# Float32 products of 256 and 272 columns in attention, scores and outputs, replaced by three float32r ones of split operands

## The chip, the cores and the metric

The kernel runs on one core of a Trainium2 chip. The metric is the time of one execution on the device, in microseconds (us); lower is better. The engines are TensorE (PE, its weight loads PEld), VectorE (DVE), ScalarE (ACT), GpSimd (POOL) and SyncE (SP, which here only issues transfers). A line L180 is line 180 of the kernel.

## The reference

It is a small decoder trunk with 272 tokens (16 meta tokens and 256 of the sequence), 2048 features, 16 heads of 128 and two layers, all in float32. Layer 0 has causal attention with a learned decay, layer 1 "stick-breaking" attention over one shared K and V; each is followed by a squared-ReLU MLP of 8192 features. In short:

```python
# layer 0
q, k, v, f = split(rms_norm(h) @ fox_w_in)
s = q @ k.T * scale + cum_logf[q] - cum_logf[k]      # masked to k <= q
o = softmax(s) @ v
h = h + o @ fox_w_o;  h = h + relu(rms_norm(h) @ w_up) ** 2 @ w_down
# layer 1
k, v = split(rms_norm(h) @ w_kv);  q = rms_norm(h) @ sb_w_q
z = q @ k.T * scale                                   # masked to k < q
a = exp(log_sigmoid(z) + suffix_sum(log_sigmoid(-z)))
o = a @ v
h = h + o @ sb_w_o;  h = h + relu(rms_norm(h) @ w_up) ** 2 @ w_down
return rms_norm(h)[meta tokens left out]
```

## The kernel before

Activations lie with features on the partitions and tokens along the columns: `hT` is 128 x 16 x 272. Almost all the work is in `gemm_group`: 512 output features, made from 16 chunks of 128 input features into four PSUM tiles `acc` (one per 128 features). To keep float32's precision with the faster format float32r, each operand is split in a high part, which is float32r, and the rest, which is float32r too; a product of two operands is then three products: high by high, high by low, low by high (L180). The activations are split once, by ScalarE and VectorE, into a `Split` (tiles `x_a`, `x_m`, `x_u`, `x_kv`, `x_o`, each with `hi` and `lo`). The weights come by DMA from SP's queue in pieces of 128 x 1024 (`raw`) and are split in the same way: ScalarE writes `whi` (L220), VectorE subtracts it and writes `wlo` (L221). There are four pairs of these buffers, so the splits run ahead of the products.

In attention the products are different: they were plain float32. The heads are taken in four groups of four.

- Layer 0, each group: a `gemm_group` for q, one for k, then the scores (L397): per head one float32 product of 144 columns for the first 128 queries and one of 272 for the others, into `ps`. VectorE adds the decay and finds the minimum (L400), ScalarE takes the exponential (L403), VectorE normalizes (L407). TensorE transposes the result (L428 to L430, `pp`), VectorE copies it out (L431, `pp_sb`). Then the `gemm_group` for v; `token_major` transposes v (L330) and ScalarE copies it (L332, `v_sb`). The output product is of 256 columns for the first 128 keys (L460), 128 columns for the next (L461) and a small one for the corners (L462); `put_split` writes the result into the Split `ao` (`x_o`), with ScalarE for the high part (L351) and VectorE for the low one (L352).
- Layer 1: q for all groups first. Each group then has a `gemm_group` for k, the scores of 256 columns (L575, `pza`) and of 144 (L576, `pzb`), the logarithms and their suffix sums (`pta`, `ptb`, already float32r with the split operands `eh` and `el`), an exponential in place (`z`), the `gemm_group` for v, and output products of 256 columns (L614) and 144 (L615).

The order is not written out by hand: the tile framework schedules the instructions of each engine by its own timeline of the program, so the small products of attention stand between the products of the next `gemm_group`. Each engine then runs its queue strictly in that order, with semaphores between engines. The tiles of attention come from the pool `att`, which lies behind all others in SBUF, and their PSUM tiles from `patt` (four banks). `tmp` has the tags `relu` and `u2` of the MLP, which are free during attention.

Of the kernel before, what the change touches and what calls it, by code (L numbers as in the profile page):

```python
# [33 lines left out]
def yoco_kernel(ctx: ExitStack, tc: tile.TileContext, hT_in, gains, b_f, w_f, w_qkv0, w_o0, w_up, w_dn,  # L34
# [264 lines left out]
    def forget_gates(rstd):  # L299
# [34 lines left out]

    def packed(src, label):

# [12 lines left out]
    def put_split(sp, h, nh, t, n, src):  # L349
        hi, lo = (x[:, h:h + nh, t - sp.t0:t - sp.t0 + n] for x in (sp.hi, sp.lo))  # L350
        nc.scalar.activation(hi, src, AF.Copy)  # L351
        nc.vector.tensor_tensor(out=lo, in0=src, in1=hi.bitcast(F32), op=ALU.subtract)  # L352

    ao = Split("o0", 0)
    for g in range(4):
# [8 lines left out]
        def evac_kv(m, acc, t):  # L364
            nc.vector.tensor_tensor(out=t[:, m, :], in0=acc, in1=box["rstd"], op=ALU.mult)
# [24 lines left out]
                   after={j: (lambda j=j: decays(j)) for j in range(4)})  # L390


        for j in range(4):
            h = 4 * g + j
            ps = patt.tile([P, 512], F32, tag="patt", name=f"ps_{h}")
            for q0, o, n in ((M, 0, 144), (M + P, 144, T)):
                nc.tensor.matmul(ps[:, o:o + n], qT[:, j, q0:q0 + P], kT[:, j, :n], start=True, stop=True)  # L397
            st = att.tile([P, 4], F32, tag="st", name=f"st_{h}")
            for i, (o, n) in enumerate(((0, 144), (144, T))):
                nc.vector.tensor_tensor_reduce(out=s[:, j, o:o + n], in0=ps[:, o:o + n], in1=s[:, j, o:o + n],  # L400
                                               scale=1.0, scalar=3.0e38, op0=ALU.add, op1=ALU.min,
                                               accum_out=st[:, i:i + 1])
                nc.scalar.activation(s[:, j, o:o + n], s[:, j, o:o + n], AF.Exp, bias=st[:, i:i + 1], scale=-1.0,  # L403
                                     accum_out=st[:, 2 + i:3 + i])
            nc.vector.reciprocal(st[:, 2:4], st[:, 2:4])
            for i, (o, n) in enumerate(((0, 144), (144, T))):
                nc.vector.tensor_scalar(s[:, j, o:o + n], s[:, j, o:o + n], st[:, 2 + i:3 + i], None, op0=ALU.mult)  # L407
# [13 lines left out]

        pps = []
        for pr in range(2):
            pp_sb = att.tile([P, 2, 416], F32, tag="pp", bufs=3, name=f"pp_sb_{g}_{pr}")
            for i in range(2):
                j = 2 * pr + i
                pp = patt.tile([P, 512], F32, tag="patt", name=f"pp_{4 * g + j}")
                nc.tensor.transpose(pp[:, 0:P], s[:, j, 0:P], ident)  # L428
                nc.tensor.transpose(pp[:, P:2 * P], s[:, j, 144:144 + P], ident)
                nc.tensor.transpose(pp[:, 2 * P:3 * P], s[:, j, 144 + P:144 + 2 * P], ident)  # L430
                nc.vector.tensor_copy(pp_sb[:, i, :3 * P], pp[:, :3 * P])  # L431
            pps.append(pp_sb)


        pm = patt.tile([P, 512], F32, tag="patt", name=f"pm_{g}")
# [18 lines left out]
        nc.tensor.matmul(po[:, :64], vm_sb[:, :P], pm_sb[:, P:], start=True, stop=True)  # L454
        put_split(ao, 4 * g, 4, 0, M, po[:, :64].rearrange("p (h q) -> p h q", h=4))
        for pr in range(2):
            v_sb = token_major(vT, pr, 0, f"0_{g}_{pr}")
            po = patt.tile([P, 2, 256], F32, tag="patt", name=f"po0_{g}_{pr}")
            for i in range(2):
                nc.tensor.matmul(po[:, i, :], v_sb[:, i, 0, :], pps[pr][:, i, 0:2 * P], start=i == 0, stop=False)  # L460
# [76 lines left out]
    ao = Split("o1", M)  # L537
    for g in range(4):
        kT = att.tile([P, 4, T], F32, tag="kT", bufs=1, name=f"kT1_{g}")
        vT = att.tile([P, 4, T], F32, tag="vT", bufs=1, name=f"vT1_{g}")  # L540
        gemm_group(w_kv[2 * g], xc, 0, lambda m, acc: evac_kv(m, acc, kT))
        q = qT1[g]

# [20 lines left out]
        sc = att.tile([P, 4, M], F32, tag="sc", name=f"sc_{g}")  # L564
        nc.vector.tensor_copy(sc, pt[:, 64:128].rearrange("p (h q) -> p h q", h=4))


        z = att.tile([P, 4, 416], F32, tag="s", bufs=1, name=f"z_{g}")
        for pr in range(2):
            zp = z[:, 2 * pr:2 * pr + 2, :400]  # L570
            pa = patt.tile([P, 2, 256], F32, tag="patt", name=f"pza_{g}_{pr}")
            pb = patt.tile([P, 2, 256], F32, tag="patt", name=f"pzb_{g}_{pr}")
            for i in range(2):
                j = 2 * pr + i
                nc.tensor.matmul(pa[:, i, :], kT[:, j, 0:P], q[:, j, :S], start=True, stop=True)  # L575
                nc.tensor.matmul(pb[:, i, :144], kT[:, j, P:2 * P], q[:, j, 112:S], start=True, stop=True)  # L576
# [4 lines left out]
            e = att.tile([P, 2, 416], F32, tag="pp", bufs=3, name=f"e_{g}_{pr}")[:, :, :400]  # L581
            e_hi = att.tile([P, 2, 416], F32R, tag="pp", bufs=3, name=f"eh_{g}_{pr}")[:, :, :400]
            e_lo = att.tile([P, 2, 416], F32R, tag="pp", bufs=3, name=f"el_{g}_{pr}")[:, :, :400]
# [7 lines left out]
            nc.tensor.matmul(pa, ntri_r, e_lo[:, :, 0:256], start=False, stop=False)  # L591
            nc.tensor.matmul(pa[:, :, 112:], nones_r, e_hi[:, :, 256:400], start=False, stop=False)
            nc.tensor.matmul(pa[:, :, 112:], nones_r, e_lo[:, :, 256:400], start=False, stop=True)
            nc.tensor.matmul(pb[:, :, :144], ntri_r, e_hi[:, :, 256:400], start=True, stop=False)
            nc.tensor.matmul(pb[:, :, :144], ntri_r, e_lo[:, :, 256:400], start=False, stop=True)
# [4 lines left out]
            nc.vector.tensor_tensor(out=zp[:, :, 256:400], in0=pb[:, :, :144], in1=zp[:, :, 256:400], op=ALU.add)  # L600
            nc.scalar.activation(zp, zp, AF.Exp)

        gemm_group(w_kv[2 * g + 1], xc, 0, lambda m, acc: evac_kv(m, acc, vT))

        pv = patt.tile([P, 512], F32, tag="patt", name=f"pvc_{g}")
# [1 line left out]
        vc_sb = att.tile([P, P], F32, tag="vm_sb", bufs=1, name=f"vc_sb_{g}")  # L607
        nc.scalar.copy(vc_sb, pv[:, :P])
        for pr in range(2):
            v_sb = token_major(vT, pr, 0, f"1_{g}_{pr}")  # L610
            po = patt.tile([P, 2, 256], F32, tag="patt", name=f"po1_{g}_{pr}")
            for i in range(2):
                j = 2 * pr + i
                nc.tensor.matmul(po[:, i, :], v_sb[:, i, 0, :], z[:, j, 0:256], start=i == 0, stop=False)  # L614
                nc.tensor.matmul(po[:, i, 112:], v_sb[:, i, 1, :], z[:, j, 256:400], start=False, stop=False)  # L615
# [112 lines left out]
```

## Time and profile before

| | |
|---|---|
| Median of 3 runs | 2301.25 us (2300.02 to 2301.27) |
| The profiled execution | 2299.54 us |
| Its span, first to last instruction | 2297.6 us |
| TensorE busy | 2286.6 us |
| VectorE, ScalarE busy | 1289.7 us, 1040.8 us |
| Granted TensorE clock, mean | 0.998 |

The profile is of one execution. A busy time is the union of an engine's records. A row of instructions by form reads: line, engine, operation, tiles (out<-in), shape, count | busy us, mean ns of one | idle time before them, and what ended it. A float32 product has two records on TensorE and two weight loads. Since products are pipelined, the records of TensorE overlap, and the mean of one is its latency. The chain of waits lists, in order of time, what the end of the program hung on; equal instructions that follow each other are one piece.

### The profile page before, as it was taken

How to read it: one execution, taken by the hardware profiler on the slowest of the kernel's cores; microseconds unless marked ns; L12 is line 12 of the kernel's file. 1: busy time of each engine (PE TensorE's matmuls, PEld its weight loads, DVE VectorE, ACT ScalarE, POOL GpSimd, SP SyncE). 2: the span in 40 equal slices, each digit the busy share in tenths (PEclk: the TensorE clock that was granted, in tenths of full speed). 3: DMA queues.
4: the chain of work that ended last, by engine and by line, in shares of the span. 5: the costliest groups of instructions: out<-in, count | busy, mean ns of one | idle time of the engine just before them, and what ended most of it. 6: DMA issues, size and time to landing. Idle time of an engine off the chain costs nothing.

```text
span 2297.6 us, 44810 instructions
## 1 busy us (share of the span) xinstructions
PE 2286.6 (100%) x19022; PEld 2280.1 (99%) x19022; DVE 1289.7 (56%) x1766; ACT 1040.8 (45%) x1397; POOL 40.2 (2%) x65
## 2 busy tenths in 40 slices
PE   9999999999999999999999999999999999999998
PEld 9999999999999999999999999999999999999998
DVE  7665555655455455455566555566555555555555
ACT  6444344543344344344445444455543543543553
POOL 1000000000000000000000000000000000000000
PEclk9999999999999999999999999999999999999999
DMA  7545555555555555555555544456566666565663
GB/s 235 175 158 166 170 162 172 168 185 175 182 175 180 180 174 184 175 183 175 177 189 188 172 147 147 147 174 198 189 192 201 186 193 202 185 201 192 193 199 133
DMA packets 116904, 412.32 MB, mean 179 GB/s; under 512 B 13520, under 2 KB 16992, under 8 KB 116704
## 3 DMA queue, kind: packets, MB, share of 16 engines
q1 hardware_dynamic: 114560, 406.29, 55.0%
q8 instruction: 149, 2.44, 0.4%
q10 hardware_dynamic: 2144, 3.17, 0.4%
q14 instruction: 51, 0.42, 0.1%
HBM read 407.29 MB, written 2.11 MB: 178 GB/s over the span
## 4 chain that ended last, share of the span: by engine, by line
PE 99%; DVE 0%; ACT 0%; issue 0%; DVEq 0%; ACTq 0%
PE acc L180 96%; PE ps L397 0%; PE pv L330 0%; PE pza L575 0%; PE po L460 0%; PE po L614 0%; PE idle L61 0%; PE po L615 0%; PE pzb L576 0%; PE po L461 0%; DVE ob L670 0%; PE pf L297 0%; PE pf L296 0%; PE pta L590 0%; PE pta L591 0%; PE pp L428 0%
## 5 line engine op out<-in xcount | busy, mean ns | idle before, releaser
L221 DVE TENSOR_TENSOR wlo<-raw,whi 128x1024 fp32r<-128x1024 f32 (+1 forms) x773 | 928.9, 1217 | 742.5 <-ACT whi L220 735.9
L220 ACT ACTIVATE whi<-raw 128x1024 fp32r<-128x1024 f32 (+1 forms) x773 | 797.3, 1050 | 1008.4 <-PE acc L180 981.1
L180 PE MATMUL acc<-x_m,whi 128*128 128x272 f32 (+1 forms) x4096 | 643.1, 281 | 0.0
L180 PE MATMUL acc<-x_u,whi 128*128 128x272 f32 (+1 forms) x4096 | 642.5, 281 | 0.0
L180 PEld LDWEIGHTS acc<-x_m,whi 128*128 128x128 f32 x4096 | 566.0, 188 | 0.1
L180 PEld LDWEIGHTS acc<-x_u,whi 128*128 128x128 f32 x4096 | 565.7, 188 | 0.0
L180 PE MATMUL acc<-x_m,wlo 128*128 128x272 f32 (+2 forms) x2048 | 440.8, 281 | 0.0
L180 PE MATMUL acc<-x_u,wlo 128*128 128x272 f32 (+2 forms) x2048 | 440.8, 281 | 0.0
L180 PE MATMUL acc<-x_a,whi 128*128 128x272 f32 (+1 forms) x2048 | 359.9, 288 | 0.0
L180 PEld LDWEIGHTS acc<-x_m,wlo 128*128 128x128 f32 x2048 | 323.4, 188 | 0.0
L180 PEld LDWEIGHTS acc<-x_u,wlo 128*128 128x128 f32 x2048 | 323.3, 188 | 0.0
L180 PEld LDWEIGHTS acc<-x_a,whi 128*128 128x128 f32 x2048 | 302.0, 189 | 0.9
L180 PE MATMUL acc<-x_a,wlo 128*128 128x272 f32 (+2 forms) x1024 | 254.0, 286 | 0.0
L180 PE MATMUL acc<-x_kv,whi 128*128 128x272 f32 x1024 | 191.8, 288 | 0.0
L180 PEld LDWEIGHTS acc<-x_a,wlo 128*128 128x128 f32 x1024 | 175.8, 189 | 0.8 <-issue 0.5
L180 PE MATMUL acc<-x_o,whi 128*128 128x272 f32 (+1 forms) x1024 | 161.9, 282 | 0.0
L180 PEld LDWEIGHTS acc<-x_kv,whi 128*128 128x128 f32 x1024 | 159.7, 188 | 0.0
L180 PE MATMUL acc<-x_kv,wlo 128*128 128x272 f32 x512 | 147.5, 288 | 0.0
L180 PEld LDWEIGHTS acc<-x_o,whi 128*128 128x128 f32 x1024 | 142.0, 188 | 0.0
L255 DVE TENSOR_TENSOR hT<-acc,hT 128x272 f32<-128x272 f32 (+1 forms) x160 | 69.0, 432 | 81.9 <-PE acc L180 81.7
L180 PE MATMUL acc<-x_o,wlo 128*128 128x272 f32 (+2 forms) x512 | 110.6, 282 | 0.0
L180 PEld LDWEIGHTS acc<-x_kv,wlo 128*128 128x128 f32 x512 | 96.5, 188 | 0.0
(225 smaller groups left out, 970.0 us busy)
## 6 DMA issues: line engine op xcount, KB each, us to landing
raw<-w_up SPq DMA_DIRECT2D x256, 512.0 KB, 4.7
raw<-w_dn SPq DMA_DIRECT2D x256, 512.0 KB, 4.7
raw<-w_qkv SPq DMA_DIRECT2D x92, 512.0 KB, 4.0
raw<-w_o SPq DMA_DIRECT2D x64, 512.0 KB, 4.3
raw<-w_kv SPq DMA_DIRECT2D x64, 512.0 KB, 3.9
raw<-w_q SPq DMA_DIRECT2D x32, 512.0 KB, 5.0
fk<-f_dram ACTq DMA_DIRECT2D x4, 544.0 KB, 4.9
raw<-w_qkv SPq DMA_DIRECT2D x7, 256.0 KB, 4.7
```

Of the source, the lines that this page charges most:

```text
L180: ins = nc.tensor.matmul(*args, **kw).ins
L220: on_act = nc.scalar.activation(hp, src, AF.Copy)
L221: on_dve = nc.vector.tensor_tensor(out=lp, in0=src, in1=hp.bitcast(F32), op=ALU.subtract)
L255: nc.vector.tensor_tensor(out=hT[:, c, t0:], in0=acc, in1=hT[:, c, t0:], op=ALU.add)
```

## The change

At four places a float32 product is replaced by three float32r products of split operands (`by_parts`): the 272-column scores of layer 0, the 256-column scores of layer 1, and the 256-column output products of both layers. `split` makes the parts: the high one on ScalarE, the rest on VectorE. The smaller float32 products (144, 128, 64 and 32 columns) stay.

- Layer 0, scores: the queries of the second block are split into `q2` (a buffer of tag `pp`), and k, head by head, into the rows of `ao` that the head's output takes later.
- Layer 0, outputs: of the transposed weights, `p0` (first 128 keys, split, straight out of PSUM) and `p1` (the others, a copy, in a tile of tag `relu`) replace `pp_sb`. `token_major` gives `v0` (split) and `v1` (a copy, in a tile of tag `u2`) in place of `v_sb`.
- Layer 1, scores: k is split into `k0`, which takes the buffer of tag `vT` until v is made, and q into the rows of `ao`.
- Layer 1, outputs: the first 256 columns of `z` are split into `p0`, which takes the buffer of k (`kT`) or of the group's queries (`qT`). The tile `vT` is allocated later, and the exponentials of both pairs of heads stand in a loop of their own.
- The buffers of tag `pp` grow from 832 to 1024 columns, which moves the `att` tiles behind them; the tiles of the other pools stay where they are.

```diff
+    def split(hl, src):
+        nc.scalar.activation(hl[:, 0], src, AF.Copy)
+        nc.vector.tensor_tensor(out=hl[:, 1], in0=src, in1=hl[:, 0].bitcast(F32), op=ALU.subtract)
+
     def token_major(vT, pr, t0, label):
...
-        v_sb = att.tile([P, 2, 2, P], F32, tag="v_sb", name=f"v_sb_{label}")
-        nc.scalar.copy(v_sb, pv)
-        return v_sb
+        v0 = att.tile([P, 2, 2, P], F32R, tag="v_sb", name=f"v0_{label}")
+        v1 = tmp.tile([P, T], F32, tag="u2", name=f"v1_{label}")[:, :2 * P].rearrange("p (i d) -> p i d", i=2)
+        split(v0, pv[:, :, 0, :])
+        nc.scalar.copy(v1, pv[:, :, 1, :])
+        return v0, v1
+
+    def by_parts(out, a, b, start, stop=False):
+        for k, (i, j) in enumerate(((0, 0), (0, 1), (1, 0))):
+            nc.tensor.matmul(out, a[i], b[j], start=start and k == 0, stop=stop and k == 2)
+
+    def weighted(po, v0, p0, i):
+        by_parts(po[:, i, :], [v0[:, k, i, :] for k in range(2)], [p0[:, k, i, :] for k in range(2)], i == 0)
...
+        q2 = att.tile([P, 2, 4, P], F32R, tag="pp", bufs=3, name=f"q2_{g}")
+        split(q2, qT[:, :, M + P:])
         for j in range(4):
...
-            for q0, o, n in ((M, 0, 144), (M + P, 144, T)):
-                nc.tensor.matmul(ps[:, o:o + n], qT[:, j, q0:q0 + P], kT[:, j, :n], start=True, stop=True)
+            put_split(ao, h, 1, 0, T, kT[:, j:j + 1, :])
+            nc.tensor.matmul(ps[:, 0:144], qT[:, j, M:M + P], kT[:, j, :144], start=True, stop=True)
+            by_parts(ps[:, 144:144 + T], [q2[:, k, j, :] for k in range(2)], [ao.hi[:, h], ao.lo[:, h]], True, True)
...
-                nc.vector.tensor_copy(pp_sb[:, i, :3 * P], pp[:, :3 * P])
-            pps.append(pp_sb)
+                split(p0[:, :, i, :], pp[:, :2 * P])
+                nc.vector.tensor_copy(p1[:, i, :], pp[:, 2 * P:3 * P])
+            pps.append((p0, p1))
...
-                nc.tensor.matmul(po[:, i, :], v_sb[:, i, 0, :], pps[pr][:, i, 0:2 * P], start=i == 0, stop=False)
-                nc.tensor.matmul(po[:, i, P:], v_sb[:, i, 1, :], pps[pr][:, i, 2 * P:3 * P], start=False, stop=False)
+                weighted(po, v0, p0, i)
+                nc.tensor.matmul(po[:, i, P:], v1[:, i, :], p1[:, i, :], start=False, stop=False)
...
+        k0 = att.tile([P, 4, T], F32R, tag="vT", bufs=1, name=f"k0_{g}")
+        k0 = k0.rearrange("p h t -> p (h t)")[:, :1024].rearrange("p (a h t) -> p a h t", a=2, h=4)
+        split(k0, kT[:, :, 0:P])
+        put_split(ao, 4 * g, 4, M, S, q[:, :, :S])
...
-                nc.tensor.matmul(pa[:, i, :], kT[:, j, 0:P], q[:, j, :S], start=True, stop=True)
+                by_parts(pa[:, i, :], [k0[:, k, j, :] for k in range(2)],
+                         [x[:, 4 * g + j] for x in (ao.hi, ao.lo)], True, True)
                 nc.tensor.matmul(pb[:, i, :144], kT[:, j, P:2 * P], q[:, j, 112:S], start=True, stop=True)
...
+        for pr in range(2):
+            zp = z[:, 2 * pr:2 * pr + 2, :400]
             nc.scalar.activation(zp, zp, AF.Exp)
-
+            p0 = att.tile([P, 4, T], F32R, tag=("kT", "qT")[pr], bufs=(1, 4)[pr], name=f"p01_{g}_{pr}")
+            p0 = p0.rearrange("p h t -> p (h t)")[:, :1024].rearrange("p (a i q) -> p a i q", a=2, i=2)
+            split(p0, zp[:, :, 0:256])
...
-                nc.tensor.matmul(po[:, i, :], v_sb[:, i, 0, :], z[:, j, 0:256], start=i == 0, stop=False)
-                nc.tensor.matmul(po[:, i, 112:], v_sb[:, i, 1, :], z[:, j, 256:400], start=False, stop=False)
+                weighted(po, v0, ps[pr], i)
+                nc.tensor.matmul(po[:, i, 112:], v1[:, i, :], z[:, j, 256:400], start=False, stop=False)
```

More of the change, by code (lines that the diff above doesn't have):

```diff
@@ L423, in yoco_kernel @@
         for pr in range(2):
-            pp_sb = att.tile([P, 2, 416], F32, tag="pp", bufs=3, name=f"pp_sb_{g}_{pr}")
+            p0 = att.tile([P, 2, 2, 256], F32R, tag="pp", bufs=3, name=f"p0_{g}_{pr}")
+            p1 = tmp.tile([P, T], F32, tag="relu", name=f"p1_{g}_{pr}")[:, :2 * P].rearrange("p (i q) -> p i q", i=2)
             for i in range(2):
@@ L456, in yoco_kernel @@
         for pr in range(2):
-            v_sb = token_major(vT, pr, 0, f"0_{g}_{pr}")
+            (v0, v1), (p0, p1) = token_major(vT, pr, 0, f"0_{g}_{pr}"), pps[pr]
             po = patt.tile([P, 2, 256], F32, tag="patt", name=f"po0_{g}_{pr}")
             for i in range(2):
-                nc.tensor.matmul(po[:, i, :], v_sb[:, i, 0, :], pps[pr][:, i, 0:2 * P], start=i == 0, stop=False)
-                nc.tensor.matmul(po[:, i, P:], v_sb[:, i, 1, :], pps[pr][:, i, 2 * P:3 * P], start=False, stop=False)
+                weighted(po, v0, p0, i)
+                nc.tensor.matmul(po[:, i, P:], v1[:, i, :], p1[:, i, :], start=False, stop=False)
             nc.tensor.matmul(po.rearrange("p i (c q) -> p (i c) q", c=2)[:, :, P - M:], vm_sb[:, P:],
@@ L565, in yoco_kernel, with pp_tile @@
         nc.vector.tensor_copy(sc, pt[:, 64:128].rearrange("p (h q) -> p h q", h=4))
+        def pp_tile(dtype, name):
+            t = att.tile([P, 2, 2, 256], dtype, tag="pp", bufs=3, name=name)
+            return t.rearrange("p a i q -> p (a i q)")[:, :832].rearrange("p (i q) -> p i q", i=2)[:, :, :400]
+        k0 = att.tile([P, 4, T], F32R, tag="vT", bufs=1, name=f"k0_{g}")
+        k0 = k0.rearrange("p h t -> p (h t)")[:, :1024].rearrange("p (a h t) -> p a h t", a=2, h=4)
+        split(k0, kT[:, :, 0:P])
+        put_split(ao, 4 * g, 4, M, S, q[:, :, :S])
         z = att.tile([P, 4, 416], F32, tag="s", bufs=1, name=f"z_{g}")
@@ L580, in yoco_kernel @@
                                     in1=maskB[:, 256:400].unsqueeze(1).to_broadcast([P, 2, 144]))
-            e = att.tile([P, 2, 416], F32, tag="pp", bufs=3, name=f"e_{g}_{pr}")[:, :, :400]
-            e_hi = att.tile([P, 2, 416], F32R, tag="pp", bufs=3, name=f"eh_{g}_{pr}")[:, :, :400]
-            e_lo = att.tile([P, 2, 416], F32R, tag="pp", bufs=3, name=f"el_{g}_{pr}")[:, :, :400]
+            e = pp_tile(F32, f"e_{g}_{pr}")
+            e_hi = pp_tile(F32R, f"eh_{g}_{pr}")
+            e_lo = pp_tile(F32R, f"el_{g}_{pr}")
             softplus(e, zp)
@@ L609, in yoco_kernel @@
         for pr in range(2):
-            v_sb = token_major(vT, pr, 0, f"1_{g}_{pr}")
+            v0, v1 = token_major(vT, pr, 0, f"1_{g}_{pr}")
             po = patt.tile([P, 2, 256], F32, tag="patt", name=f"po1_{g}_{pr}")
```

4 lines of the change are left out of this document (3 added, 1 removed).

## The prediction

> **What bounds the kernel now.** First the page: the busy time of each engine, the chain that ended last, then the waits of TensorE.
>
> ```profile
> span 2297.6 us, 44810 instructions
> PE 2286.6 (100%) x19022; PEld 2280.1 (99%) x19022; DVE 1289.7 (56%) x1766; ACT 1040.8 (45%) x1397; POOL 40.2 (2%) x65
> PEclk9999999999999999999999999999999999999999
> PE 99%; DVE 0%; ACT 0%; issue 0%; DVEq 0%; ACTq 0%
> ```
>
> ```profile
> PE pr_fin L659 <- DVE fin L653: 1.3, 1, 1.3
> PE idle L61 <- DVE mean_w L57: 1.1, 1, 1.1
> PE pms_fin L627 <- ACT sq_fin L639: 0.2, 1, 0.2
> ```
>
> TensorE is 99% of the chain, at full clock, and waited three times in all, 2.6 us, each time at an end of the program. In between every product stands in line behind another. So two questions decide this change: how much TensorE time the products give back, and whether something that was hidden comes to hold TensorE up.
>
> A busy row can't price a product: it gives the latency of each record, and records overlap. What a product costs the line is the distance from start to start. The chain of waits gives that, as the length of runs of equal products. Its columns are start us, us, what.
>
> ```profile
> 59.23 1.41 PE ps L397 x8
> 98.84 0.43 PE po L460 x2
> 105.46 33.85 PE acc L180 x274
> 1305.40 0.24 PE pzb L576 x2
> 1305.64 0.43 PE pza L575 x2
> 1317.55 0.23 PE pta L591
> 1317.78 0.13 PE pta L592
> 1317.91 0.13 PE pta L593
> 1318.05 0.14 PE ptb L595
> 1332.33 0.43 PE po L614 x2
> 1332.76 0.25 PE po L615 x2
> 1598.97 686.20 PE acc L180 x6048
> ```
>
> A float32 product stands there as two records. One of 256 columns takes 0.43 us, at all three places (L460, L575, L614). One of 144 columns takes 0.24 or 0.25 (L576, L615), so 0.245. The eight records at 59.23 are two heads with 144 and 272 columns each, so one of 272 takes (1.41 - 2 x 0.245) / 2 = 0.46 us. A float32r product is one record: 33.85 / 274 = 0.1235 us with 272 columns, 686.20 / 6048 = 0.1135 us with 256.
>
> **The change, part by part.** These are the products that go, by form (shape, count of records, busy us, mean ns):
>
> ```profile
> L397 PE MATMUL ps<-kT,qT 128*128 128x272 f32 x32 | 9.9, 392 | 0.0
> L575 PE MATMUL pza<-qT,kT 128*128 128x256 f32 x32 | 9.7, 386 | 0.0
> L460 PE MATMUL po<-pp_sb,v_sb 128*128 128x256 f32 x32 | 9.5, 379 | 0.0
> L614 PE MATMUL po<-z,v_sb 128*128 128x256 f32 x32 | 9.5, 379 | 0.0
> ```
>
> Two records each, so 16 products of each line: 16 of 272 columns, 48 of 256.
>
> 1. *272 columns (ps).* 0.46 us goes, 3 x 0.1235 = 0.3705 comes: 0.09 us saved, times 16 = 1.43 us.
> 2. *256 columns (pza, po twice).* 0.43 goes, 3 x 0.1135 = 0.3405 comes: 0.09 saved, times 48 = 4.30 us.
> 3. *The rate is the uncertain part of both.* These float32r operands lie elsewhere in SBUF than those of L180. The nearest rows with such tiles are the four from 1317.55: 512 + 3 x 288 = 1376 columns in 0.63 us, the next instruction starting at 1318.18, 0.458 ns a column against 0.443 in the 256-column run at L180. At 0.458, 256 columns take 0.117 us, 272 take 0.125, and the parts save 1.36 + 3.8 = 5.2 us instead of 5.7. I take L180's rates, the same kind of work in the greatest number, and keep 5.2.
> 4. *More changes between float32 and float32r.* The smaller float32 products (144, 128 columns) stay and now stand alone between float32r ones. In the built order TensorE changes kind 278 times instead of 214. What one change costs:
>
> ```profile
> 144.22 0.38 PE L410 MATMUL ps<-kT,pk_qm 128*128 128x128 f32 x2
> 144.35 0.50 PE L180 MATMUL acc<-x_a,whi 128*128 128x272 f32 x2
> 144.69 0.29 PE L180 MATMUL acc<-x_a,wlo 128*128 128x272 f32 x1
> ```
>
> From 144.22 to 144.69 stand a 128-column float32 product (0.22, half of 256) and two of L180 (0.247): 0.467 expected, 0.47 measured. So a few ns for two changes; I take 3 ns for one, 64 x 3 = 0.2 us lost, at most 10 ns, 0.6 us.
>
> Sum on TensorE: 1.43 + 4.30 - 0.2 = 5.5 us less, with bounds 4.6 (5.2 - 0.6) and 5.9.
>
> The Trainium skill ("TensorE: Matmul & The Clock Gate", Back-to-back issue gap) gives N / 2.4 + 2.5 ns for an isolated product, so 109 ns for 256 columns and 116 for 272. By it the parts would save about 6.7 us. The float32r runs here go at 113.5 and 123.5 ns, so the rows hold and the page's figure is no end of my range.
>
> 5. *The splits, on ScalarE and VectorE.* New: in each layer 0 group q2 (512 columns), four rows of kT (272), four p0 (256, in place of part of the 384-column copy), two v0; in each layer 1 group q (1024), k0 (512), two p0 (512), two v0. None is on TensorE; each is free while its product stands far enough behind it. Prices from like forms:
>
> ```profile
> L352 DVE TENSOR_TENSOR x_o<-po,x_o 128x512 fp32r<-128x512 f32 x16 | 11.0, 690 | 15.2 <-ACT x_o L351 15.2
> L496 DVE TENSOR_TENSOR x_u<-u,x_u 128x272 fp32r<-128x272 f32 x64 | 27.9, 436 | 1.7
> L496 DVE TENSOR_TENSOR x_u<-u,x_u 128x256 fp32r<-128x256 f32 x64 | 25.4, 417 | 0.0
> L431 DVE COPY pp_sb<-pp 128x384 f32<-128x384 f32 x16 | 8.8, 550 | 0.3
> L439 DVE TENSOR_TENSOR pm_sb<-pm,maskD 128x128 f32<-128x128 f32 x4 | 1.1, 282 | 0.4 <-PE pm L437 0.4
> L221 DVE TENSOR_TENSOR wlo<-raw,whi 128x1024 fp32r<-128x1024 f32 x764 | 923.1, 1224 | 739.7 <-ACT whi L220 733.1
> L220 ACT ACTIVATE whi<-raw 128x1024 fp32r<-128x1024 f32 x764 | 792.1, 1056 | 1005.3 <-PE acc L180 981.1 <-ACT sq_m L155 6.4 <-issue 6.0
> ```
>
> VectorE in layer 0: 0.69 + 4 x 0.436 + 4 x (0.417 + 0.28 - 0.55) + 2 x 0.417 = 3.9 us a group; in layer 1: 1.22 + 3 x 0.69 + 2 x 0.417 = 4.1 us. ScalarE's additions are about as long, and it has more room (45% against 56%). What hides them over the whole is in the last two rows: VectorE's weight splits wait for ScalarE's (733 us in all) and those wait for TensorE to give back a buffer (981 us). The pairs of split weights run ahead of their use: there are four pairs, and one lasts TensorE 24 x 0.1235 = 3.0 us, so with one in use and one being split (1.06 + 1.22 us) there are about 6 us of cushion. SP issues the same transfers in the same order, and POOL's queue is unchanged, so nothing new stands in those.
>
> The tight place is where scores are made in layer 0 (the first row, of busy time by stretch; the second is the same work of layer 1):
>
> ```profile
> 140.00:151.00 11.00, 11.00 (x87) 10.77 (x86) 10.34 (x39) 6.98 (x21) 0.44 (x2) 1.00 0.30 98
> 1304.00:1320.00 16.00, 16.00 (x124) 15.70 (x123) 10.40 (x17) 8.35 (x11) 0.00 (x0) 1.00 0.51 165
> ```
>
> In layer 0 VectorE (third engine in the row) is busy 10.34 of 11.00 us, and kT's splits and p0 bring 2.4 more. Its strict queue: a softmax step waits behind kT's lower part. The row that tells the room is the first transposition of a head's weights (pp), which needs its softmax done:
>
> ```profile
> 139.35 0.44 DVE L365 TENSOR_TENSOR kT<-acc,rstd_a 128x272 f32<-128x272 f32 x1 [1.04 <-PE acc L180]
> 143.35 0.56 DVE L407 TENSOR_SCALAR s<-s,st 128x144 f32<-128x144 f32 x2
> 146.06 0.27 PE L428 MATMUL pp<-ident,s 128*128 128x128 f32 x1
> ```
>
> Softmax is done at 143.91, 4.56 us after kT's last eviction began, and TensorE gets there at 146.06: 2.15 us to spare. In the changed order VectorE has one kT split (0.44) and a second reciprocal (0.16) more in that stretch: 5.2 us, done at 144.5. And the products' order is changed with it: the transposition now stands 7.6 us of TensorE work behind the first score instead of 6.9, at 139.16 + 7.6 = 146.8. To spare: 2.2 us. The last head's transposition stands 15.3 us behind instead of 11.2. In layer 1 VectorE has over 5 us free in 16; only the four q splits stand together, ahead of the first K group, 4 x 1.22 = 4.9 us, which the cushion of 6 covers. So I cost the splits at nothing; without that cover in layer 0, all of VectorE's 3.1 us there (q2 included) would come four times, 12.4 us.
>
> 6. *Buffers.* p0 of layer 1 takes kT's buffer, so the next group's kT waits for the last output product:
>
> ```profile
> 1339.12 17.98 PE acc L180 x145
> ```
>
> Behind that product TensorE still has 18 us of projection before the next scores, and kT's evictions come in its last 6 us: 12 us to spare. k0 takes vT's buffer, read long before.
>
> **Sum.** The profiled execution took 2299.54 us, 1.9 more than its span; less 5.5 is 2294.0. The median of the runs is 2301.25, so the forecast is 2301.25 - 5.5 = 2295.8 us, 0.24% faster. About 0.2%, 4.6 us, is what a measurement of this kernel can tell from no change, so this lies just beyond.
>
> **The rivals.**
>
> *The rate eats the gain.* If a float32r product from these tiles is slower than any row shows, or a few waits of some tenths come in, the gain falls under 4.6 us. By itself the rate must be 0.47 ns a column or worse (0.120 us for 256). For: no row has just these tiles. Against: the slowest row is 0.458. Time: a gain of 3.6, 2297.6 us.
>
> *VectorE holds up the scores.* If its queue is late at the transpositions, TensorE waits in each of the four groups of layer 0. For: 10.34 of 11.00 us busy. Against: the 2.2 us to spare, and the later places of the transpositions. Price at worst 12.4 us: 2301.25 - 5.5 + 12.4 = 2308.2. It makes the kernel slower by over 0.2% from 2.5 us of waiting a group ((5.5 + 4.6) / 4), so VectorE would have to be 4.7 us later than worked out.
>
> *The third weight load isn't hidden.* A float32 product has two loads, three float32r ones have three.
>
> ```profile
> L180 PEld LDWEIGHTS acc<-x_m,whi 128*128 128x128 f32 x4096 | 566.0, 188 | 0.1
> ```
>
> A load takes 0.188 us; one more per product exposed is 64 x 0.188 = 12.0 us, so 2307.8. Against: these 4096 products start 0.12 us apart, less than one load, so loads do run beside products.
> The Trainium skill speaks for this rival ("TensorE: Matmul & The Clock Gate", Part 3, "What overlaps and what doesn't"): a load overlaps a running product only if it aims at another row group, and all of these use the whole array. The trace doesn't agree, as the 0.188 beside 0.12 shows.
>
> **How the numbers follow.** Forecast 0.73; rate eats the gain 0.18; VectorE 0.06; weight load 0.03. Faster by over 0.2% is the first, within 0.2% the second, slower by over 0.2% the last two: 0.73, 0.18, 0.09. The range goes from the best gain, 5.9, with the 1.2 us by which the runs of before lie apart (2294.1), to a gain of 2.6, which takes in most of the second case: 2298.7.
>
> **What would show it.** Right: runs of three float32r products at 0.34 (256) and 0.37 us (272) in the chain of waits where 0.43 and 0.46 stood; TensorE's waits still 2.6 us, all at the ends; VectorE's busy time up by 4 x 3.9 + 4 x 4.1 = 32 us or somewhat less, with no effect. Wrong: waits of TensorE for VectorE at pp or ps (then the order is too tight), a rate over 0.125 us for 256 columns, or L180's own runs no longer at 0.1235 and 0.1135, of which a hundredth would outweigh all of this: 18432 products of some 0.12 us, 22 us. The tiles of L180 lie at the same addresses as before.

## The result, and the profile after

| | before | after |
|---|---|---|
| Median of 15 runs each | 2300.41 us (2299.1 to 2301.27) | 2295.52 us (2294.72 to 2297.41) |
| The profiled execution | 2299.54 us | 2294.73 us |
| Its span | 2297.6 us | 2293.0 us |

After takes 0.9979 of the time of before, with a 95% interval of 0.9973 to 0.9986: 4.9 us less, 0.21%. The forecast was 5.5 us less. It was made from the median of the first three runs, 2301.25; from the median of all fifteen it would have been 2294.9. One execution below was slow, the second of e2_shift with 4894.71 us, and is left out.

First the page of after: busy times, and the chain that ended last, by engine.

```profile
span 2293.0 us, 45093 instructions
PE 2281.7 (100%) x19086; PEld 2278.7 (99%) x19086; DVE 1315.9 (57%) x1834; ACT 1065.7 (46%) x1465; POOL 39.8 (2%) x65
PE 99%; DVE 0%; DMA 0%; ACT 0%; SPq 0%; issue 0%; DVEq 0%; ACTq 0%
```

The kernel is still bound by TensorE. VectorE and ScalarE have 26 and 25 us more to do, and their shares hardly move. The waits of TensorE in after say whether that work holds it up anywhere (the columns behind the colon: us in total, times, longest).

```profile
PE pr_fin L699 <- DVE fin L693: 1.3, 1, 1.3
PE idle L61 <- DVE mean_w L57: 1.1, 1, 1.1
PE acc L180 <- ACT whi L220: 0.3, 1, 0.3
PE pms_fin L667 <- ACT sq_fin L679: 0.2, 1, 0.2
```

Three are the waits of before, at the ends. The fourth, 0.3 us for a split weight, comes just before 7.3 us, long before the first changed product at 59. No product of attention waits for a split. So the time was won in the products, and the chain of waits gives their lengths, by the distance from the start of a run to the start of what follows. In after:

```profile
59.13 0.24 PE ps L416 x2
...
138.91 0.38 PE ps L345 x3
...
436.78 756.84 PE acc L180 x6144
...
1303.15 0.36 PE pza L345 x3
1303.51 0.24 PE pzb L607 x2
...
1330.72 0.35 PE po L345 x3
...
1594.35 686.20 PE acc L180 x6048
```

A triple of 272 columns takes 0.38 us where 0.46 stood. A triple of 256 takes 0.35 or 0.36 where 0.43 stood. The float32 products of 144 columns between them are as long as before (0.24), and so are the two long runs at L180 (756.84 and 686.20): the rest of TensorE's work kept its rate to a hundredth of a us in 757.

The long runs also mark the stages. In before the first of them, the MLP of layer 0, begins here:

```profile
439.19 756.84 PE acc L180 x6144
```

The first score starts at 59.23 in before and at 59.13 in after. From there to the MLP layer 0 takes 439.19 - 59.23 = 379.96 us, and after the change 377.65: 2.31 saved. From the end of that run to the next one, layer 1 takes 402.94 and then 400.73: 2.21 saved. Behind that nothing changes. So the two halves give back nearly the same, as 32 changed products in each should, and the 4.5 us together are the gain of the two profiled spans, 4.6, but for 0.1 us at the start. The medians lie 4.9 apart; that differs from 4.6 by less than the runs of one kernel do among themselves.

Not every triple stays together: in TensorE's order 29 of the 64 (13 of `ps`, 16 of `po`) are parted by other products, nearly always of L180.

### The profile page after: what moved, and what is told of

Same layout as the page of the kernel before. It is cut to its first block, busy times and chain, and to the rows that moved or that the text cites. A ratio compares the mean times of both kernels' runs of the same rounds, so it can differ in the third digit from the quotient of the medians.

```text
span 2293.0 us, 45093 instructions
## 1 busy us (share of the span) xinstructions
PE 2281.7 (100%) x19086; PEld 2278.7 (99%) x19086; DVE 1315.9 (57%) x1834; ACT 1065.7 (46%) x1465; POOL 39.8 (2%) x65
## 4 chain that ended last, share of the span: by engine, by line
PE 99%; DVE 0%; DMA 0%; ACT 0%; SPq 0%; issue 0%; DVEq 0%; ACTq 0%
PE acc L180 96%; PE po L345 0%; PE pv L335 0%; PE ps L345 0%; PE pza L345 0%; DMA raw<-w_qkv 0%; PE po L655 0%; PE pzb L607 0%; PE ps L416 0%; PE po L483 0%; DVE ob L710 0%; PE pf L297 0%; PE pf L296 0%; PE pta L621 0%; PE pta L622 0%; PE pp L451 0%
## 5 line engine op out<-in xcount | busy, mean ns | idle before, releaser
L180 PE MATMUL acc<-x_m,whi 128*128 128x272 f32 (+1 forms) x4096 | 643.0, 281 | 0.0
L180 PE MATMUL acc<-x_u,whi 128*128 128x272 f32 (+1 forms) x4096 | 642.5, 281 | 0.0
L180 PEld LDWEIGHTS acc<-x_m,whi 128*128 128x128 f32 x4096 | 565.9, 188 | 0.1
L180 PEld LDWEIGHTS acc<-x_u,whi 128*128 128x128 f32 x4096 | 565.7, 188 | 0.0
L180 PE MATMUL acc<-x_m,wlo 128*128 128x272 f32 (+2 forms) x2048 | 440.8, 281 | 0.0
L180 PE MATMUL acc<-x_u,wlo 128*128 128x272 f32 (+2 forms) x2048 | 440.8, 281 | 0.0
L180 PE MATMUL acc<-x_a,whi 128*128 128x272 f32 (+1 forms) x2048 | 357.9, 286 | 0.3 <-ACT whi L220 0.3
L180 PEld LDWEIGHTS acc<-x_m,wlo 128*128 128x128 f32 x2048 | 323.3, 188 | 0.0
L180 PEld LDWEIGHTS acc<-x_u,wlo 128*128 128x128 f32 x2048 | 323.3, 188 | 0.0
L180 PEld LDWEIGHTS acc<-x_a,whi 128*128 128x128 f32 x2048 | 301.5, 188 | 0.8 <-ACT whi L220 0.5
L180 PE MATMUL acc<-x_a,wlo 128*128 128x272 f32 (+2 forms) x1024 | 254.5, 286 | 0.0
L180 PE MATMUL acc<-x_kv,whi 128*128 128x272 f32 x1024 | 193.4, 288 | 0.0
L180 PEld LDWEIGHTS acc<-x_a,wlo 128*128 128x128 f32 x1024 | 175.5, 188 | 0.5 <-issue 0.5
L180 PE MATMUL acc<-x_o,whi 128*128 128x272 f32 (+1 forms) x1024 | 162.8, 282 | 0.0
L180 PEld LDWEIGHTS acc<-x_kv,whi 128*128 128x128 f32 x1024 | 160.0, 188 | 0.0
L180 PE MATMUL acc<-x_kv,wlo 128*128 128x272 f32 x512 | 146.8, 287 | 0.0
L180 PEld LDWEIGHTS acc<-x_o,whi 128*128 128x128 f32 x1024 | 142.2, 188 | 0.0
L180 PE MATMUL acc<-x_o,wlo 128*128 128x272 f32 (+2 forms) x512 | 110.9, 282 | 0.0
L180 PEld LDWEIGHTS acc<-x_kv,wlo 128*128 128x128 f32 x512 | 96.4, 188 | 0.1
```

The costliest lines, as they stand in the source:

```text
L180: ins = nc.tensor.matmul(*args, **kw).ins
```

## The experiments

The experiments ask three things: are the splits free, are the products what pays, and why does a product in a triple take 0.118 us when L180's take 0.1135? The diffs are against the changed kernel, but for e4_fp32s, which is made from the one before. The experiments ran on three chips, on which the kernel before has medians of 2300.02 to 2301.12 us, so half a microsecond between two kernels' times says little; the stages within the profiles say more. Stages are measured as above: layer 0 from the first score to the first long run, layer 1 from the end of that run to the start of the second.

### The splits alone (e5_splits)

Every split is made, into tiles that no product reads, and the products stay float32.

```diff
+    def unread(src, tag, label):
+        hi, lo = (tmp.tile([P, T], F32R, tag=tag, name=f"{x}_{tag}_{label}")[:, :2 * P] for x in ("hi", "lo"))
...
+        nc.scalar.activation(hi, src, AF.Copy)
+        nc.vector.tensor_tensor(out=lo, in0=src, in1=hi.bitcast(F32), op=ALU.subtract)
...
-            by_parts(ps[:, 144:144 + T], [q2[:, k, j, :] for k in range(2)], [ao.hi[:, h], ao.lo[:, h]], True, True)
+            nc.tensor.matmul(ps[:, 144:144 + T], qT[:, j, M + P:M + 2 * P], kT[:, j, :T], start=True, stop=True)
```

> All the splits of the change are made, but no product reads them: the four products stay float32 (and the old copies are made too, so VectorE and ScalarE have some 5 us more than in the changed kernel). Theory 'cover': ScalarE's and VectorE's work is hidden, so the time is that of the kernel before, 2300.4, within 1 us, and TensorE has no new waits. Rival 'VectorE holds up the scores': part of the 32 us that VectorE gets is seen, 2303 or more, with waits at the transpositions (pp) or scores (ps).

Measured: 2299.59 us against 2300.35 of before on the same chip, ratio 0.9997 (0.9988 to 1.0005). Its chain of waits has the long runs at the places of before (439.19 and 1598.97):

```profile
439.11 756.84 PE acc L180 x6144
...
1598.79 686.20 PE acc L180 x6048
```

VectorE is busy 1321.9 us there, 32 more than in before, and TensorE's waits are the three at the ends. So the splits cost nothing that can be measured, and the whole gain is the products'.

### Four times the subtraction of k (e6_dve)

The lower part of each row of k is computed four times: 48 more instructions of VectorE, ahead of the softmax steps that the transpositions need.

```diff
             put_split(ao, h, 1, 0, T, kT[:, j:j + 1, :])
+            for _ in range(3):
+                nc.vector.tensor_tensor(out=ao.lo[:, h], in0=kT[:, j], in1=ao.hi[:, h].bitcast(F32), op=ALU.subtract)
```

> The changed kernel with the subtraction that makes the lower part of kT done four times per head in place of once: VectorE gets 3 x 4 x 0.436 = 5.2 us more in each of layer 0's four score stretches, 21 us in all. Theory 'cover': the order is planned with it and the transpositions move back again, so TensorE waits little, 2295.5 to 2297. Rival 'VectorE holds up the scores': the 2.2 us to spare are used up and each group loses about 3 us, 2307 or so.

Measured: 2296.2 us, ratio to before 0.9983 (0.9973 to 0.9993). By form VectorE's added work is this row:

```profile
L417 DVE TENSOR_TENSOR x_o<-kT,x_o 128x272 fp32r<-128x272 f32 x48 | 19.9, 434 | 0.1
```

These are the waits of TensorE, all of them:

```profile
PE pr_fin L701 <- DVE fin L695: 1.3, 1, 1.3
PE idle L61 <- DVE mean_w L57: 1.1, 1, 1.1
PE pms_fin L669 <- ACT sq_fin L681: 0.2, 1, 0.2
```

48 x 0.434 = 20.8 us, 5.2 a group, is more than the 2.2 us that the prediction had to spare, and still TensorE does not wait. The timeline of TensorE says why, with the first score and the first transposition of the second group of heads (start us, us):

```profile
139.37 0.41 PE L418 MATMUL ps<-kT,qT 128*128 128x144 f32 x2
...
150.34 0.27 PE L451 MATMUL pp<-ident,s 128*128 128x128 f32 x1
```

The scheduler has moved the transposition further back. It starts 11.0 us after the first score here, 7.7 in after (146.19 less 138.50) and 6.9 in before (146.06 less 139.16), always with TensorE busy in between. So the room is not fixed: the order is made anew for each kernel, and it puts other products ahead of one whose operand comes late. What a late VectorE would do in an order that stays as it is was not tested. Layer 0 takes 438.39 - 59.78 = 378.61 us in this profile, 0.96 more than in after. No wait accounts for that; the other order may, but this is not shown.

### Five triples (e3_triples), and five float32 products (e4_fp32s)

Both repeat the same 64 products four times more, the one in the changed kernel as triples, the other in the kernel before as float32 products. The repeats write what was there, so the output stays. In layer 1 the 144-column product is repeated as well, so that a repeat alternates between the two.

```diff
+            for _ in range(4):
+                by_parts(ps[:, 144:144 + T], [q2[:, k, j, :] for k in range(2)], [ao.hi[:, h], ao.lo[:, h]], True, True)
...
+                for _ in range(4):
+                    by_parts(pa[:, i, :], [k0[:, k, j, :] for k in range(2)],
+                             [x[:, 4 * g + j] for x in (ao.hi, ao.lo)], True, True)
+                    by_parts(pb[:, i, :144], [k0[:, k, j, :] for k in range(2)],
+                             [x[:, 4 * g + j, 112:S] for x in (ao.hi, ao.lo)], True, True)
```

> The changed kernel with four more triples ahead of each of the 272-column triples (ps) and 256-column triples (pza), and four more triples of 144 columns ahead of each 144-column float32 product (pzb); the last product starts its sum anew, so the outputs stay. That is 64 more triples of each of the three sizes. At the changed kernel's own spacing (0.126 us for 272, 0.119 for 256) the first two add 64 x 0.378 + 64 x 0.357 = 47.0 us; if the slow part were only at the borders with float32, 64 x (0.371 + 0.341) = 45.6. The 144-column triples: by columns alone at 0.46 ns, 64 x 0.199 = 12.7 us, 0.066 us a product, which would make them cheaper than a float32 product of 144 (0.245); if the weight load sets a floor (the load of 128 columns must fit in), 0.11 us or more a product, 0.33 a triple, 21 us, and splitting the small products would lose time.

```diff
-            for q0, o, n in ((M, 0, 144), (M + P, 144, T)):
+            for q0, o, n in ((M, 0, 144),) + ((M + P, 144, T),) * 5:
...
-                nc.tensor.matmul(pa[:, i, :], kT[:, j, 0:P], q[:, j, :S], start=True, stop=True)
-                nc.tensor.matmul(pb[:, i, :144], kT[:, j, P:2 * P], q[:, j, 112:S], start=True, stop=True)
+                for _ in range(5):
+                    nc.tensor.matmul(pa[:, i, :], kT[:, j, 0:P], q[:, j, :S], start=True, stop=True)
+                    nc.tensor.matmul(pb[:, i, :144], kT[:, j, P:2 * P], q[:, j, 112:S], start=True, stop=True)
```

> The kernel before with each 272-column score product of layer 0 and each 256- and 144-column one of layer 1 made five times in place of once (the last starts its sum anew, so the outputs stay). The prediction's terms: 64 x 0.458 + 64 x 0.431 + 64 x 0.245 = 72.6 us more than before, about 2373. If the borders made part of the price of a single product, less.

Measured: 2364.73 us with the triples, ratio to before 1.028 (1.026 to 1.0301), and 2371.82 with the float32 products, 1.0311 (1.0291 to 1.0332). That is 71.8 us more than before for the float32 products (72.6 expected), and 69.2 more than after for the triples (47 and 21 expected, if products of 144 columns take 0.11 us or more). The chain of waits of the first, and then of the second:

```profile
59.92 0.24 PE ps L416 x2
...
461.35 756.84 PE acc L180 x6144
...
1327.77 0.40 PE pza L345 x3
1328.17 0.29 PE pzb L345 x3
...
1663.28 686.20 PE acc L180 x6048
```

```profile
59.45 10.15 PE ps L397 x48
...
468.41 756.84 PE acc L180 x6144
...
1671.49 686.20 PE acc L180 x6048
```

Each stage has 64 repeats. With triples layer 0 takes 401.43 us, 23.8 more than after: 0.372 us for a triple of 272 columns. With float32 it takes 408.96, 29.0 more than before: 0.453 for a product. Layer 1 takes 445.09 with triples, 44.4 more: 0.693 for a pair of triples of 256 and 144 columns, 0.40 + 0.29 in the rows. With float32 it takes 446.24, 43.3 more: 0.677 for a pair, where the rows of before gave 0.43 + 0.245 = 0.675.

So the 272-column product gains 0.453 - 0.372 = 0.081 us. The 256-column one gains 0.43 - 0.355 = 0.075 by the rows of after (0.35 and 0.36). 16 x 0.081 + 48 x 0.075 = 4.9 us. The stages together gave back 4.5, so about 0.4 us was lost again outside these rows, and that this sum equals the 4.9 between the medians is chance.

In layer 1 the pair lost instead, 0.693 against 0.677. With the 256-column product alone split, as in after, the pair takes 0.36 + 0.24 = 0.60. If the 256-column triple is 0.355 here too, three products of 144 columns take 0.338, 0.113 each; inside these triples the starts stand 109 and 112 ns apart on average. That is hardly less than with 256 columns, and the float32 product of 0.245 is cheaper. Splitting the smaller products as well would therefore have cost time. What sets this spacing is not shown; one candidate is the weight load of 128 columns that each product brings. The Trainium skill ("TensorE: Matmul & The Clock Gate", LDWEIGHTS (loading the stationary operand)) gives a load its columns / 1.2 ns, 107 ns for 128. The spacing lies just above that, while the records of such loads in these traces last 0.188 us, so the page's figure is not seen by itself.

### Another place in SBUF (e2_shift, e1_align)

The tiles of `gemm_group` have an offset of 16 columns, 64 bytes, where the activations begin at the 16th token (`o = 16 if t0 else 0`). That suggested that the place of the two operands relative to each other matters. By the addresses that the tiles get, which no trace shows, the stationary operand less the moving one, modulo 256 bytes, is 64 in those runs, and 160 (`pza`), 0 (`po`) and 224 (`ps`) in the triples of after. The first kernel takes the offset away from `gemm_group`; the second gives the operands of all triples the 64 bytes.

```diff
-                o = 16 if t0 else 0
+                o = 0
```

> The changed kernel with the split weights of the 256-column gemm groups (layer 1) moved back by 64 bytes, so that they stand 0 instead of 64 bytes from the moving operand modulo 256, as v0 and p0 do in the triples. Theory 'place': the long runs of 256 columns go from 0.1134 to about 0.1175 us a product, 7560 x 0.0041 = 31 us more, about 2326. Rival 'neighbours': these runs are long and have no float32 product beside them, so nothing changes, 2295.5.

```diff
+        v0 = att.tile([P, 576], F32R, tag="v_sb", name=f"v0_{label}")
+        v0 = v0[:, 16:528].rearrange("p (a i d) -> p a i d", a=2, i=2)
...
+        q2 = att.tile([P, 1088], F32R, tag="pp", bufs=3, name=f"q2_{g}")
+        q2 = q2[:, 24:1048].rearrange("p (a h q) -> p a h q", a=2, h=4)
...
-        k0 = k0.rearrange("p h t -> p (h t)")[:, :1024].rearrange("p (a h t) -> p a h t", a=2, h=4)
+        k0 = k0.rearrange("p h t -> p (h t)")[:, 40:1064].rearrange("p (a h t) -> p a h t", a=2, h=4)
```

> The changed kernel with the stationary operands of the triples moved by a few bytes in SBUF (v0 by 64, q2 by 96, k0 by 160 bytes), so that stationary and moving operand stand 64 bytes apart modulo 256, as they do in the gemm groups (L180). The order of TensorE's instructions is the same. Theory 'place': a float32r product is slower where the two operands stand otherwise; triples of 256 columns go from about 0.358 to 0.341 us, of 272 from 0.378 to 0.371, so 48 x 0.017 + 16 x 0.007 = 0.9 us less than the changed kernel, about 2294.6. Rival 'neighbours': the triples are slow because they are short and stand between float32 products; then nothing changes, 2295.5.

Measured without the offset: 2343.8 us in one run, 48 more than after. Its chain of waits has the two long runs, the first of which (layer 0) keeps its weights' place, as

```profile
437.70 757.41 PE acc L180 x6144
...
1605.13 724.51 PE acc L180 x6048
```

The products of the second run take 0.1198 us each, where 0.1135 stood: the same instructions and the same tiles, with the weights 64 bytes aside. (0.1175 was expected; the effect is larger.) The first run, untouched, keeps its length to 0.1%. So the rate of float32r products does depend on their place. Whether it is the distance between the two operands that counts, or the place of the weights alone, this doesn't tell, since only the weights moved; nor did any run try another modulus than 256.

Measured with the offset in the triples: 2294.99 us, ratio to before 0.9976 (0.9966 to 0.9985). That is 0.5 us under after, and the intervals lie over each other. Its chain of waits, where after has 0.36 at `pza`:

```profile
59.77 0.24 PE ps L418 x2
...
437.31 756.83 PE acc L180 x6144
...
1303.67 0.35 PE pza L346 x3
...
1594.66 686.20 PE acc L180 x6048
```

Layer 0 takes 377.54 us and layer 1 400.52, together 0.3 less than in after. At L180's rate each of the 48 triples of 256 columns would be 14 ns shorter. From the last float32 record ahead of a whole triple to the first one behind it, start to start, the mean went from 482 to 477 ns at `pza` (between two `pzb` products) and from 471 to 473 at `po`. So the place explains at most a small part of why triples of three are slow.

The float32 neighbours are not needed for it either. Where a triple of `po` is parted, its products stand alone between float32r products of L180, as here in after:

```profile
1335.27 0.12 PE po L345
1335.39 0.63 PE acc L180 x5
1336.03 0.12 PE po L345
```

The 24 such single products of after take 117 to 121 ns, 119 on average, no less than those in whole triples. In e1_align they take 120. What is left is that the runs are short.

### Runs of 27 instead of 3 (e8_long, e9_long_aligned)

In layer 1 each triple of the scores is computed nine times over, in after and in e1_align; the repeats again write what was there.

```diff
             for i in range(2):
                 j = 2 * pr + i
+                for _ in range(8):
+                    by_parts(pa[:, i, :], [k0[:, k, j, :] for k in range(2)],
+                             [x[:, 4 * g + j] for x in (ao.hi, ao.lo)], True, True)
```

> The changed kernel with eight more 256-column triples straight ahead of each one of pza, so runs of 27 float32r products with no float32 product among them (the last triple starts its sum anew, the outputs stay): 128 more triples, 384 products. Theory 'place': the operands stand 160 bytes apart modulo 256, so the products stay at about 0.1185 us however long the run, 45.5 us more than the changed kernel, 2341.0. Theory 'short run': in a long run they reach the 0.1134 us of the gemm groups, 43.5 us more, 2339.1.

> The same long runs with the moved operands of e1_align, 64 bytes apart modulo 256. Theory 'place' and theory 'short run' both say 0.1134 us a product, 43.5 us more than e1_align, 2338.5; if it stays at 0.118, neither distance nor length is what the gemm groups have and these lack.

Measured: 2341.38 us and 2339.48, each with 16 x 24 = 384 products more. The chains of waits, first without, then with the 64 bytes:

```profile
437.14 756.84 PE acc L180 x6144
...
1306.39 3.24 PE pza L345 x27
...
1640.94 686.20 PE acc L180 x6048
```

```profile
437.57 756.83 PE acc L180 x6144
...
1306.66 3.09 PE pza L346 x27
...
1323.61 3.18 PE pza L346 x27
...
1639.29 686.20 PE acc L180 x6048
```

The expectations were 2341.0 (by place) and 2338.5. Layer 1 is 46.2 us longer than in after and 44.4 longer than in e1_align: 0.120 and 0.116 us a product. Inside the runs the difference is plain. These are the distances from one start to the next, in ns, in a run of the first pair of heads, behind its first few products:

```
e8_long          117 125 116 123 118 121 117 125 116 123 118 121 ...
e9_long_aligned  113 113 114 113 113 114 113 113 114 ...
```

With the 64 bytes a long run reaches the 0.1135 of L180, after up to five slower products of 116 to 124 ns; without them it doesn't in 27 products. So neither the length alone (e8_long) nor the place alone (e1_align) gives that rate; together they gave it in three of each group's four runs. In the fourth they did not, which fits neither theory: with the 64 bytes too, the last run of the second pair of heads stays at 117 to 119 ns (3.18 / 27 = 0.118), in every group. Its operands stand at the same distance. Other engines are not the reason: beside that run VectorE and ScalarE are idle and no transfer runs, in all four groups (1323.60 to 1326.80 in the first), while the fast run from 1306.70 has transfers beside it. Why it stays slow is open.

### Two triples together (e7_grouped)

In e1_align a float32 product follows each triple. Here the triples of two heads stand together and their float32 products behind them, so that `pza`'s runs are of six. TensorE changes kind 34 times less in the trace (244 against 278), not some 48.

```diff
             for i in range(2):
                 j = 2 * pr + i
                 by_parts(pa[:, i, :], [k0[:, k, j, :] for k in range(2)],
                          [x[:, 4 * g + j] for x in (ao.hi, ao.lo)], True, True)
+            for i in range(2):
+                j = 2 * pr + i
                 nc.tensor.matmul(pb[:, i, :144], kT[:, j, P:2 * P], q[:, j, 112:S], start=True, stop=True)
```

> e1_align, and in pza/pzb and both output products the triples of the two heads of a pair stand together in the source, then their float32 products, so TensorE changes between the two kinds some 48 times less. At 3 ns a change that is 0.15 us; if a change costs 10 ns, 0.5 us. Theory 'place' alone: as e1_align, about 2294.5. Rival 'neighbours': 1 us or more below e1_align.

Measured: 2295.79 us, ratio to before 0.9979 (0.997 to 0.9988), 0.8 above e1_align and 0.3 above after, all within the intervals. In the chain a run of six behind float32r products takes 0.71 us, still 0.118 a product. The gain that was looked for did not come. No version that was run beats after by more than can be measured.

## Why the prediction was right, and where a term was off

The time came out 0.3 us from the forecast, 2295.5 against 2295.8, and so near is luck: the gain was put 0.6 us too high, and the median of three runs that it was taken from lay 0.8 us above that of fifteen. The mechanism is what holds.

**What bounds the kernel**: right. TensorE is 99% of the chain in both profiles, and what changed is the length of 64 products.

**Steps 1 and 2, the products**: the right mechanism, the size too large, and step 2 is the term that was mis-sized. A float32 product of 256 columns was forecast to turn into 3 x 0.1135 = 0.3405 us; it turned into 0.355. So step 2 gave 48 x 0.075 = 3.6 us instead of 4.30. Step 1 gave 16 x 0.081 = 1.3 instead of 1.43. The upper bound of 5.9 doesn't follow from the prediction's terms, which without any loss give 1.43 + 4.30 = 5.7.

**Step 3, the rate**: here was the choice that made the difference. It had L180's rate, from many thousand products, and 0.458 ns a column from four products of attention, and took the first. The second gives 0.117 and 0.125 us; measured are 0.118 and 0.124 to 0.126. The row with fewer instructions was the nearer one. What it shares with the triples is the short run: its four products stand between float32r products of L180, and so do the parted triples, which are as slow as the whole ones. The reason that the prediction gave, that the operands lie elsewhere, is a true cause of such a difference (e2_shift), but it made up little of it here (e1_align).

**Step 4, the changes of kind**: not measured apart. TensorE changes kind 278 times in the trace, as forecast. What the stages lack to the sum of the rows, 4.9 - 4.5 = 0.4 us, is all that can be laid to these 64 changes: about 6 ns each instead of 3, within the bound of 10. Whether they are its cause is not shown. A dearer change of kind is not what makes up the 14 ns of a triple: inside the whole 256-column triples of after the starts stand 116 to 121 ns apart, so each product is slower, and grouping the triples (e7_grouped) brought nothing back.

**Step 5, the splits**: right, with the trace close to its working. These rows of VectorE in after, by form, stand against its prices:

```profile
L368 DVE TENSOR_TENSOR x_o<-kT,x_o 128x272 fp32r<-128x272 f32 x16 | 6.9, 439 | 2.2 <-ACT x_o L367 1.8
L328 DVE TENSOR_TENSOR p<-z,p 128x512 fp32r<-128x512 f32 x8 | 5.5, 683 | 0.0
L368 DVE TENSOR_TENSOR x_o<-qT,x_o 128x1024 fp32r<-128x1024 f32 x4 | 4.6, 1219 | 0.0
```

0.439, 0.683 and 1.219 us, against 0.436, 0.69 and 1.22. All in all VectorE is busy 26 us more, against 32 "or somewhat less". The tight place, first VectorE and then TensorE in the timeline of after (start us, us):

```profile
138.70 0.44 DVE L381 TENSOR_TENSOR kT<-acc,rstd_a 128x272 f32<-128x272 f32 x1
143.11 1.04 DVE L427 TENSOR_SCALAR s<-s,st 128x144 f32<-128x144 f32 x4
```

```profile
138.50 0.41 PE L416 MATMUL ps<-kT,qT 128*128 128x144 f32 x2
...
146.19 0.27 PE L449 MATMUL pp<-ident,s 128*128 128x128 f32 x1
```

The four softmax steps are two heads; the first head's end at about 143.7, 5.0 us after kT's last eviction began (5.2 forecast), and TensorE comes to the transposition at 146.19, 7.7 us after the first score (7.6 forecast): 2.5 us to spare (2.2 forecast). In the stretch from 140 to 151, VectorE, third engine in the row, is busy less than the 10.34 us of before, not more; the work of the scores begins earlier and ends later now (the last head's transposition comes at 153.88 instead of 150.31), so part of it falls outside:

```profile
140.00:151.00 11.00, 11.00 (x92) 11.00 (x91) 9.33 (x36) 7.38 (x25) 0.00 (x0) 1.00 0.34 109
```

**Step 6, the buffers**: right; no wait stands there. TensorE's waits are 2.9 us instead of the 2.6 that the prediction named as a sign, by the 0.3 us at 7.3 us, which no changed product has a part in.

**The rivals.** "The rate eats the gain" came half true: the rate is worse than forecast, 0.46 ns a column in place of 0.443, but short of the 0.47 from which the gain falls under 4.6 us. The gain of 4.9 lies just beyond that bound, and its interval (0.14% to 0.27%, 3.2 to 6.2 us) reaches to both sides, so forecast and rival can't be told apart by the time alone. "VectorE holds up the scores" is refuted by TensorE's waits in after and by e5_splits; with 5.2 us more a group (e6_dve) it still doesn't come, there because the scheduler adds room where the prediction counted on a fixed one. "The third weight load isn't hidden" is refuted by the products themselves. By form, the loads of `pza` in after:

```profile
L345 PEld LDWEIGHTS pza<-x_o,k 128*128 128x128 f32 x48 | 6.9, 189 | 0.2
```

A load's record lasts 0.189 us, and three products with three such loads take 0.36 together (1303.15 in the chain above). The rule cited with that rival, that a load overlaps a running product only in another row group (the Trainium skill, "TensorE: Matmul & The Clock Gate", Part 3, "What overlaps and what doesn't"), does not hold for the triples either.

## What to carry to other kernels

Price a product by the distance from start to start in runs that resemble its own: as long, and at the same place; a rate from thousands of equal products is the best case. Work given to engines with room is free only while the order leaves them time, and where a scheduler makes the order, ask what it will move, not only what room the old order has. Three float32r products instead of a float32 one paid here at 256 and 272 columns (0.355 against 0.43 us, 0.372 against 0.453) and would not at 144 (0.338 against 0.245).

## What the runs showed of the hardware

- The rate of long runs of float32r products depends on where their operands lie: 0.1135 us for 256 columns with 64 bytes, modulo 256, between the stationary and the moving operand, 0.1198 with 0 (e2_shift), 0.120 with 160 (e8_long). One run in four with 64 bytes stayed at 0.118 (e9_long_aligned). Only the stationary operand was moved, so its own place may be what counts. In runs of three it made 0.3 to 0.5 us in all, within the intervals (e1_align). Which part of the chip this comes from no run shows.
- A float32r product of 256 columns in a short run is slower than in a long one, 117 to 121 ns against 113.5, also where it stands alone between other float32r products (after).
- A float32r product hardly gets cheaper below 256 columns: 0.109 to 0.113 us with 144 (e3_triples).
- A float32 product costs roughly by its columns: 0.245 us (144), 0.43 (256), 0.453 (272), so splitting it pays only above some width between 144 and 256.
